# The FFN down product of a 1280-token layer: twenty output tiles of 22 blocks each, or seven block products

## The chip, the cores and the metric

The kernel runs on one core of one Trainium2 chip. The metric is the time of one execution on the device in microseconds (us). Engines are named as in the profile: PE is TensorE's matmul, PEld its weight load, DVE VectorE, ACT ScalarE, POOL GpSimd, SP the engine on whose queue the kernel puts its DMAs.

## The reference

One encoder layer and a final norm, for two sequences of 256 and 1024 tokens, 1280 tokens in all, of width 1024, in fp32:

```
h = _rmsnorm(x, norm_mix_g);  proj = h @ w_in
y_hy = _hyena(...);  y_att = _attention(...)
x = x + concat(norms of both) @ w_out
h = _rmsnorm(x, norm_ffn_g)
x = x + (silu(h @ w_gate) * (h @ w_up)) @ w_down
return _rmsnorm(x, final_norm_g)
```

w_gate and w_up are 1024 x 2816, w_down is 2816 x 1024. The change concerns the last product, the residual add and the final norm, and what of the gate/up stage feeds them.

## The kernel before

Every matmul operand is split into a high and a low part of a reduced fp32 format (`F32R`). `mm3` (line 178) makes one fp32 product of three matmuls: high by high (line 180), high by low (181), low by high (182). A split is a cast on ScalarE for the high part and a subtract for the low part, by the helper `tt` (line 173), on GpSimd where G is passed and on VectorE otherwise.

The layer up to w_out takes the span up to about 890 us; the change does not touch it. It leaves the residual sum of each of ten 128-token tiles in DRAM (`x2d`), and its normed form in SBUF.

The gate/up stage (lines 1220 to 1326) computes h @ w_gate and h @ w_up together by seven block products (Winograd's form of Strassen's scheme): `right_side` transposes the tokens and makes the seven right factors, kept in SBUF for all 1280 tokens; `left_side(n)` loads four 256 KB pieces of the weights for column block n of 22, makes four sums on GpSimd and splits seven left factors; `gate_up(n)` runs seven keys, each over two token chunks of 256 and 384 columns, four contraction blocks of three matmuls, and folds each result into the buffers s, g, t, u of 128x640 (640 tokens are one half of each token pair). At the end t and u hold the activations of one column block for the two token halves and go to DRAM in `actd` (line 1323).

The down stage (lines 1332 to 1383) runs two halves h of the 1024 output columns. For h it loads 22 blocks of w_down of 128x512 (`load_down`, raw in three buffers, 24 split ones), and for each of ten token tiles the activations of all 22 blocks from `actd` (`load_act`, two pieces of 11 blocks, 704 KB each). One PSUM bank collects 22 x 3 matmuls. VectorE then adds the residual, ScalarE squares with a row sum, and in the second half GpSimd makes the row's factor, VectorE scales both halves and SP stores them.

PSUM has eight banks in one rotating tag (`bank`, line 1217). The order of instructions on each engine's queue is fixed when the program is built, by a scheduler that runs over the program text in order and may move an instruction ahead of earlier ones where its model of the time has it ready sooner; at run time each queue is strictly in order. Inside `opened` pools a tag has a fixed number of rotating buffers, and a new tile waits for the readers of the one whose buffer it takes.

Of the kernel before, what the change touches and what calls it, by code (L numbers as in the profile page):

```python
# [11 lines left out]
F32 = mybir.dt.float32  # L12
F32R = mybir.dt.float32r
AF = mybir.ActivationFunctionType
ALU = mybir.AluOpType
# [10 lines left out]
NF = FF // 128  # L26
# [3 lines left out]
EPS = 1e-6  # L30
# [7 lines left out]
MUL, ADD, SUB = ALU.mult, ALU.add, ALU.subtract  # L38
# [77 lines left out]
def hymba_layer_kernel(ctx: ExitStack, tc: tile.TileContext, A, dbg=None):  # L116
    nc = tc.nc
    dbg = dbg or {}
    V, S, G, T, Q = nc.vector, nc.scalar, nc.gpsimd, nc.tensor, nc.sync

    cst = ctx.enter_context(tc.tile_pool(name="cst", bufs=1))
    drm = ctx.enter_context(tc.tile_pool(name="drm", bufs=1, space=DRAM))

    def opened(name, side=None, **kw):

        st = ExitStack()
        if side:
            kw["side"] = side
        return st.enter_context(tc.tile_pool(name=name, bufs=1, reuse_waits="tile", **kw)), st.close
# [12 lines left out]
    s2, r2, s1, fh = pool("s2", 8), pool("r2", 3), pool("s1", 5), pool("fh", 2)  # L142
    ca, cb, c8, t3, sm = pool("ca", 2), pool("cb", 2), pool("c8", 2), pool("t3", 2), pool("sm", 6)
# [25 lines left out]
    def stt(out, in0, scalar, in1, op0=MUL, op1=ADD, eng=None):  # L169
        (eng or V).scalar_tensor_tensor(out=out, in0=in0, scalar=scalar, in1=in1, op0=op0, op1=op1)  # L170

    def tt(out, in0, in1, op, eng=None):
        return (eng or V).tensor_tensor(out=out, in0=in0, in1=in1, op=op)  # L173

    def f(ap):
        return ap.bitcast(F32)

    def mm3(out, lh, ll, rh, rl, first, last):

        T.matmul(out=out, lhsT=lh, rhs=rh, start=first, stop=False)  # L180
        T.matmul(out=out, lhsT=lh, rhs=rl, start=False, stop=False)  # L181
        T.matmul(out=out, lhsT=ll, rhs=rh, start=False, stop=last)  # L182
# [5 lines left out]
    one = cst.tile([128, 2], F32, name="one")  # L188
    V.memset(one, 1.0)
    ones = one[:, 0:1].broadcast_to([128, 128])  # L190
    mhalf = cst.tile([128, 8], F32, name="mhalf")
# [28 lines left out]
    x1d = [drm.tile([128, 1024], F32, name=f"x1d{i}") for i in range(10)]  # L220
    x2d = [drm.tile([128, 1024], F32, name=f"x2d{i}") for i in range(10)]

    actd = drm.tile([2, 5, 128, NF, 128], F32, name="actd")
    dft = {}

    anchor = [None]
# [286 lines left out]
    def o_rows(i):  # L513
        return A["y_sample"][0, i * 128:(i + 1) * 128, :] if i < 8 else A["y_prompt"][0, (i - 8) * 128:(i - 7) * 128, :]
# [702 lines left out]
    def bank(name):  # L1217
        return psf.tile([128, 512], F32, name=name, tag="bank", bufs=8)
# [44 lines left out]
    def left_side(n):  # L1263

        cs = slice(n * 128, (n + 1) * 128)
        raw = {}
        for nm, src, k0 in (("a11", wg, 0), ("a12", wg, 4), ("a21", wu, 0), ("a22", wu, 4)):
            raw[nm] = wo0.tile([128, 4, 128], F32, name=nm, tag=nm)
            Q.dma_start(out=raw[nm], in_=src[:, k0:k0 + 4, cs])

        def parts(key, x, of):
            w = of.tile([128, 2, 4, 128], F32R, name="w" + key, tag="w" + key)
            S.copy(out=w[:, 0], in_=x)  # L1273
            tt(w[:, 1], x, f(w[:, 0]), SUB, G)
            return w

        def combo(x, y, op):
            t = wo1.tile([128, 4, 128], F32, name="ws", tag="ws", bufs=3)
            tt(t, x, y, op, G)
            return t  # L1280

        A_ = {"b11": parts("b11", raw["a11"], wo0), "b21": parts("b21", raw["a12"], wo0)}
        s1_ = combo(raw["a21"], raw["a22"], ADD)
        s2_ = combo(s1_, raw["a11"], SUB)
        A_["s2"] = parts("s2", s2_, wo0)
        A_["s3"] = parts("s3", combo(raw["a11"], raw["a21"], SUB), wo1)
        A_["s1"] = parts("s1", s1_, wo1)
        A_["b22"] = parts("b22", combo(raw["a12"], s2_, SUB), wo1)
        A_["t4"] = parts("t4", raw["a22"], wo1)
        return A_  # L1290

    def gate_up(n, by_chunk):
        W = left_side(n)
        v = {x: wo1.tile([128, 640], F32, name=f"v{x}", tag=f"v{x}", bufs=2) for x in "sgtu"}
        steps = [(c, key) for c in range(2) for key in RIGHT] if by_chunk else \
            [(c, key) for key in RIGHT for c in range(2)]
        for c, key in steps:
            c0, w = CW2[c]
            p = bank("prod")[:, 0:w]
            for k in range(4):  # L1300
                mm3(p, W[key][:, 0, k], W[key][:, 1, k], B[key][0][c][:, k], B[key][1][c][:, k], k == 0, k == 3)
            s, g, t, u = (v[x][:, c0:c0 + w] for x in "sgtu")
            if key == "b11":
                S.copy(out=s, in_=p)
            elif key == "b21":
                tt(g, p, s, ADD)
                S.activation(out=g, in_=g, func=AF.Silu)
            elif key == "s2":
                tt(s, p, s, ADD)
            elif key == "s3":  # L1310
                tt(t, p, s, ADD)
            elif key == "s1":
                tt(u, p, t, ADD)
                tt(s, p, s, ADD)
            elif key == "b22":
                tt(s, p, s, ADD)
                S.activation(out=s, in_=s, func=AF.Silu)
                tt(u, s, u, MUL)
            else:
                tt(t, t, p, SUB)  # L1320
                tt(t, g, t, MUL)
        for x, half in (("u", 1), ("t", 0)):
            Q.dma_start(out=actd[half, :, :, n].rearrange("j p t -> p j t"), in_=v[x].rearrange("p (j t) -> p j t", j=5))

    for n in range(NF):
        gate_up(n, n == 0)
    wo1_close()
    wo0_close()
    bt_close()


    dn, dn_close = opened("dn")
    gl = dn.tile([128, 1024], F32, name="gl", tag="gl")
    Q.dma_start(out=gl, in_=A["final_norm_g"].rearrange("(o d) -> o d", o=1).broadcast_to([128, 1024]))
    y0, ms0 = {}, {}

    def load_down(n, h):
        raw = dn.tile([128, 512], F32, name="draw", tag="draw", bufs=3)
        Q.dma_start(out=raw, in_=A["w_down"][0, n * 128:(n + 1) * 128, h * 512:(h + 1) * 512])
        w = dn.tile([128, 2, 512], F32R, name="wd", tag="wd", bufs=24)  # L1340
        S.copy(out=w[:, 0], in_=raw)  # L1341
        tt(w[:, 1], raw, f(w[:, 0]), SUB, G)
        return w

    def load_act(half, j):
        raw = dn.tile([128, NF, 128], F32, name="araw", tag="araw", bufs=2)
        a = dn.tile([128, 2, NF, 128], F32R, name="act", tag="act", bufs=2)
        for m in range(0, NF, 11):
            ms = slice(m, m + 11)
            Q.dma_start(out=raw[:, ms], in_=actd[half, j, :, ms])  # L1350
            S.copy(out=a[:, 0, ms], in_=raw[:, ms])  # L1351
            tt(a[:, 1, ms], raw[:, ms], f(a[:, 0, ms]), SUB)
        return a

    for h in range(2):
        hs = slice(h * 512, (h + 1) * 512)
        W = None
        for j in range(5):
            for half in range(2):
                i = 2 * pairs[j] + half  # L1360
                a = load_act(half, j)
                if W is None:
                    W = [load_down(n, h) for n in range(NF)]
                p = bank("dn")
                for n in range(NF):
                    mm3(p, a[:, 0, n], a[:, 1, n], W[n][:, 0], W[n][:, 1], n == 0, n == NF - 1)
                if h == 0:
                    y = y0[i] = dn.tile([128, 512], F32, name="y0", tag="y0", bufs=10)
                    ms0[i] = dn.tile([128, 2], F32, name="ms", tag="ms", bufs=10)
                else:  # L1370
                    y = dn.tile([128, 512], F32, name="y1", tag="y1", bufs=2)
                Q.dma_start(out=y, in_=x2d[i][:, hs])
                tt(y, p, y, ADD)
                junk = dn.tile([128, 512], F32, name="yj", tag="yj", bufs=1)
                S.activation(out=junk, in_=y, func=AF.Square, accum_out=ms0[i][:, h:h + 1])
                if h == 1:
                    r = dn.tile([128, 1], F32, name="yr", tag="yr", bufs=2)
                    tt(r, ms0[i][:, 0:1], ms0[i][:, 1:2], ADD, G)
                    G.tensor_scalar(out=r, in0=r, scalar1=1.0 / 1024, scalar2=EPS, op0=MUL, op1=ADD)
                    tt(r, r, mhalf[:, 0:1], ALU.pow, G)  # L1380
                    for z, (yy, zs) in enumerate(((y0[i], slice(0, 512)), (y, hs))):
                        stt(yy, yy, r, gl[:, zs], MUL, MUL)
                        Q.dma_start(out=o_rows(i)[:, zs], in_=yy)
    dn_close()
    psf_close()

# [23 lines left out]
```

## Time and profile before

| | us |
|---|---|
| median of three runs | 1813.91 (1812.72 to 1815.08) |
| profiled execution | 1812.55 |
| its span in the profile | 1810.3 |
| PE busy | 1654.0 (91%) |
| POOL busy | 853.7 (47%) |
| DVE busy | 963.4 (53%) |
| ACT busy | 717.8 (40%) |
| mean granted TensorE clock | 0.956 of full |

The span is what the trace covers; 2.25 us lie around it. Busy time of an engine is a sum over its instructions, and its share is an average over stages. A releaser is the instruction whose semaphore ended a wait. Matmul durations in the trace overlap, so the rate of matmuls is read from the distance of repeating events.

### The profile page before, as it was taken

To read this page: it belongs to the slowest core of one execution; us is meant where nothing else is said; L and a number is where in the kernel's file an instruction comes from. 1 tells how busy PE (TensorE), PEld (TensorE's weight loads), DVE (VectorE), ACT (ScalarE), POOL (GpSimd) and SP (SyncE) were. 2 spreads that over 40 slices of the span, in tenths; PEclk is the share of its full clock that TensorE was granted. 3 is DMA by queue.
4 is the path that set the end of the run, shared out by engine and by line. 5 is a ranking of instruction groups with operands and counts; after the bars stand their busy time and mean duration, and the time that the engine had idled before them with its cause. 6 is when DMAs were issued, how large, how long until landed. Compare 5 with 4: busy or idle time off the path is not lost.

```text
span 1810.3 us, 25721 instructions
## 1 busy us (share of the span) xinstructions
PE 1654.0 (91%) x9737; PEld 1472.9 (81%) x9737; DVE 963.4 (53%) x1514; ACT 717.8 (40%) x1331; POOL 853.7 (47%) x771
## 2 busy tenths in 40 slices
PE   6999999988796879988699999999999958999998
PEld 4777789977785868876589999999999946888786
DVE  6559889768878765564554333334333331222432
ACT  5444443336676675463342222222222223223321
POOL 5134465632778753333576555555565415005210
PEclk9899999989898979999799999999999979999999
DMA  7453445524342433332222222222222175224441
GB/s 267 150 175 104 141 136 154 169 77 129 105 140 81 125 95 136 109 143 80 73 62 64 69 71 76 65 77 69 64 76 71 41 265 179 96 96 162 156 142 58
DMA packets 158565, 205.75 MB, mean 114 GB/s; under 512 B 10960, under 2 KB 114568, under 8 KB 158283
## 3 DMA queue, kind: packets, MB, share of 16 engines
q1 hardware_dynamic: 158203, 196.25, 33.5%
q0 software_dynamic: 240, 7.86, 1.2%
q8 instruction: 77, 1.26, 0.3%
q14 instruction: 45, 0.37, 0.1%
HBM read 158.20 MB, written 53.74 MB: 117 GB/s over the span
## 4 chain that ended last, share of the span: by engine, by line
PE 44%; DMA 4%; POOL 1%; DVE 1%; ACT 1%; issue 0%; SPq 0%; POOLq 0%; DVEq 0%; ACTq 0%
PE prod L182 10%; PE prod L181 10%; PE prod L180 10%; PE dn L182 5%; PE dn L181 5%; PE dn L180 4%; DMA draw<-in_w_down 3%; POOL wd L173 1%; DMA y<-x2d 0%; ACT wd L1341 0%; PE tp L1236 0%; PE wo L182 0%; PE wo L180 0%; DVE xx L170 0%; PE wo L181 0%
## 5 line engine op out<-in xcount | busy, mean ns | idle before, releaser
L180 PE MATMUL dn<-wd,act 128*128 128x512 f32 x440 | 173.4, 400 | 22.2 <-ACT wd L1341 19.5
L181 PE MATMUL dn<-wd,act 128*128 128x512 f32 x440 | 176.5, 401 | 3.0 <-POOL wd L173 2.8
L182 PE MATMUL dn<-wd,act 128*128 128x512 f32 x440 | 175.3, 399 | 1.9 <-DVE act L173 1.9
L173 POOL TENSOR_TENSOR wd<-draw,wd 128x512 fp32r<-128x512 f32 x44 | 59.9, 1381 | 179.0 <-ACT wd L1341 175.6
L173 DVE TENSOR_TENSOR y<-dn,y 128x512 f32<-128x512 f32 x20 | 13.7, 691 | 216.6 <-PE dn L182 175.3
L1351 ACT CAST act<-araw 128x1408 fp32r<-128x1408 f32 x40 | 52.9, 1371 | 171.0 <-PE dn L182 157.9
L180 PEld LDWEIGHTS dn<-wd,act 128*128 128x128 f32 x440 | 85.0, 194 | 42.4 <-ACT wd L1341 21.1
L811 PE MATMUL pt<-ident,P 128*128 128x128 f32 x544 | 85.6, 287 | 34.2 <-DVE PT L173 25.7
L173 DVE TENSOR_TENSOR PT<-pt,PT 128x512 fp32r<-128x512 f32 x136 | 92.6, 685 | 38.4 <-ACT PT L814 37.9
L173 POOL TENSOR_TENSOR ws<-ws,ws 128x512 fp32r<-128x512 f32 x66 | 85.4, 1295 | 55.5 <-ACT ws L1273 55.5
L173 DVE TENSOR_TENSOR vs<-prod,vs 128x256 f32<-128x256 f32 (+1 forms) x132 | 64.4, 488 | 88.1 <-PE prod L182 88.1
L1273 ACT CAST ws<-ws 128x512 fp32r<-128x512 f32 x66 | 41.0, 621 | 168.9 <-PE prod L182 164.7
L814 ACT CAST PT<-pt 128x512 fp32r<-128x512 f32 x136 | 79.6, 589 | 67.8 <-PE pt L811 66.3
L181 PEld LDWEIGHTS dn<-wd,act 128*128 128x128 f32 x440 | 84.7, 192 | 26.5 <-POOL wd L173 9.4
L811 PEld LDWEIGHTS pt<-ident,P 128*128 128x128 f32 x544 | 66.3, 147 | 47.1 <-DVE PT L173 28.0
L182 PEld LDWEIGHTS dn<-wd,act 128*128 128x128 f32 x440 | 84.9, 193 | 20.0 <-DVE act L173 2.7
L828 PE MATMUL ro<-PT,V 128*128 128x256 f32 x544 | 81.2, 305 | 10.4 <-DVE PT L173 7.8
L828 PEld LDWEIGHTS ro<-PT,V 128*128 128x128 f32 x544 | 75.7, 209 | 16.2 <-DVE PT L173 10.5
L173 POOL TENSOR_TENSOR ws<-a,a 128x512 f32<-128x512 f32 x44 | 56.8, 1290 | 62.5 <-DMA a<-in_w_up 62.4
L796 DVE TENSOR_REDUCE nm<-s 128x1 f32<-128x1024 f32 (+1 forms) x68 | 82.4, 1212 | 4.4 <-PE s L792 2.7
L800 ACT ACTIVATE P<-s,nm 128x1024 f32<-128x1024 f32 (+1 forms) x80 | 79.5, 1001 | 9.8 <-DVE nm L796 9.7
L173 DVE TENSOR_TENSOR vg<-prod,vs 128x256 f32<-128x256 f32 (+1 forms) x44 | 21.6, 491 | 115.3 <-PE prod L182 114.8
(405 smaller groups left out, 5437.2 us busy)
## 6 DMA issues: line engine op xcount, KB each, us to landing
araw<-actd SPq DMA_DIRECT2D x40, 704.0 KB
tabf<-dft SPq DMA_DIRECT2D x40, 384.0 KB
a<-in_w_gate SPq DMA_DIRECT2D x44, 256.0 KB
a<-in_w_up SPq DMA_DIRECT2D x44, 256.0 KB
draw<-in_w_down SPq DMA_DIRECT2D x44, 256.0 KB
wraw<-in_w_in SPq DMA_DIRECT2D x36, 256.0 KB
dft<-in_dft POOLq DMA_DIRECT2D x5, 1536.0 KB, 9.5
tabs<-dft SPq DMA_DIRECT2D x20, 384.0 KB
```

The costliest lines, as they stand in the source:

```text
L173: return (eng or V).tensor_tensor(out=out, in0=in0, in1=in1, op=op)
L180: T.matmul(out=out, lhsT=lh, rhs=rh, start=first, stop=False)
L181: T.matmul(out=out, lhsT=lh, rhs=rl, start=False, stop=False)
L182: T.matmul(out=out, lhsT=ll, rhs=rh, start=False, stop=last)
L796: V.tensor_reduce(out=nm, in_=sf.rearrange("p (g k) -> p g k", g=n), axis=AX.X, op=ALU.max, negate=True)
L800: S.activation(out=P[:, ks], in_=sf[:, ks], func=AF.Exp, bias=nm[:, g:g + 1], accum_out=un["rs"][:, g, b:b + 1])
L811: T.transpose(out=pt[:, t * 128:(t + 1) * 128], in_=P[:, (t0 + t) * 128:(t0 + t + 1) * 128], identity=ident)
L814: S.copy(out=dh, in_=pv)
L828: T.matmul(out=o, lhsT=vt, rhs=PT[:, hl, t0 + n], start=n == 0 and hl == 0, stop=n == len(ts) - 1 and hl == 1)
L1273: S.copy(out=w[:, 0], in_=x)
L1351: S.copy(out=a[:, 0, ms], in_=raw[:, ms])
```

## The change

The down product too is computed with seven block products. The contraction (22 blocks) is halved into j and 11 + j, the tokens into the two halves, the output columns into two of 512. After each pair of column blocks j, 11 + j `down_left` makes four sums of activation blocks on VectorE and stores seven left factors of 128x640 per j to DRAM (`ad`), and `down_right` loads the four quarters of w_down's blocks in two column pieces of 256, makes four differences on GpSimd and stores them to DRAM (`td`). In gate/up two sums are made in place, the s and g buffers are single and the sums' buffers two. The down stage runs seven products; each loads, for each of 11 contraction blocks, one right factor of 128x512 and one left factor of 128x640, splits both, and runs five token tiles of three matmuls into five PSUM banks, the contraction index outermost. The last product has the token tile outermost. The results are folded into five 128x512 buffers each of s, g, t, u; the residual is added on GpSimd.

```diff
@@ -220,7 +220,9 @@
     x1d = [drm.tile([128, 1024], F32, name=f"x1d{i}") for i in range(10)]
     x2d = [drm.tile([128, 1024], F32, name=f"x2d{i}") for i in range(10)]
 
-    actd = drm.tile([2, 5, 128, NF, 128], F32, name="actd")
+    KD = NF // 2
+    ad = {o: drm.tile([KD, 128, 640], F32, name=f"ad{o}") for o in ("a11", "a12", "a22", "s1", "s2", "s3", "s4")}
+    td = {o: drm.tile([KD, 128, 512], F32, name=f"td{o}") for o in ("t1", "t2", "t3", "t4")}
     dft = {}
 
     anchor = [None]
@@ -1274,8 +1276,8 @@
             tt(w[:, 1], x, f(w[:, 0]), SUB, G)
             return w
 
-        def combo(x, y, op):
-            t = wo1.tile([128, 4, 128], F32, name="ws", tag="ws", bufs=3)
+        def combo(x, y, op, out=None):
+            t = wo1.tile([128, 4, 128], F32, name="ws", tag="ws", bufs=2) if out is None else out
             tt(t, x, y, op, G)
             return t
 
@@ -1283,15 +1285,15 @@
         s1_ = combo(raw["a21"], raw["a22"], ADD)
         s2_ = combo(s1_, raw["a11"], SUB)
         A_["s2"] = parts("s2", s2_, wo0)
-        A_["s3"] = parts("s3", combo(raw["a11"], raw["a21"], SUB), wo1)
+        A_["s3"] = parts("s3", combo(raw["a11"], raw["a21"], SUB, raw["a21"]), wo1)
         A_["s1"] = parts("s1", s1_, wo1)
-        A_["b22"] = parts("b22", combo(raw["a12"], s2_, SUB), wo1)
+        A_["b22"] = parts("b22", combo(raw["a12"], s2_, SUB, s2_), wo1)
         A_["t4"] = parts("t4", raw["a22"], wo1)
         return A_
 
     def gate_up(n, by_chunk):
         W = left_side(n)
-        v = {x: wo1.tile([128, 640], F32, name=f"v{x}", tag=f"v{x}", bufs=2) for x in "sgtu"}
+        v = {x: wo1.tile([128, 640], F32, name=f"v{x}", tag=f"v{x}", bufs=2 if x in "tu" else 1) for x in "sgtu"}
         steps = [(c, key) for c in range(2) for key in RIGHT] if by_chunk else \
             [(c, key) for key in RIGHT for c in range(2)]
         for c, key in steps:
@@ -1319,68 +1321,159 @@
             else:
                 tt(t, t, p, SUB)
                 tt(t, g, t, MUL)
-        for x, half in (("u", 1), ("t", 0)):
-            Q.dma_start(out=actd[half, :, :, n].rearrange("j p t -> p j t"), in_=v[x].rearrange("p (j t) -> p j t", j=5))
-
-    for n in range(NF):
-        gate_up(n, n == 0)
+        return v["t"], v["u"]
+
+    def down_left(j, one, two):
+
+        (a11, a21), (a12, a22) = one, two
+
+        def sum_(x, y, op, key, out=None):
+            t = wo1.tile([128, 640], F32, name="vx", tag="vx", bufs=2) if out is None else out
+            tt(t, x, y, op)
+            Q.dma_start(out=ad[key][j], in_=t)
+            return t
+
+        for key, x in (("a11", a11), ("a12", a12), ("a22", a22)):
+            Q.dma_start(out=ad[key][j], in_=x)
+        x1_ = sum_(a21, a22, ADD, "s1")
+        x2_ = sum_(x1_, a11, SUB, "s2")
+        sum_(a11, a21, SUB, "s3", a21)
+        sum_(a12, x2_, SUB, "s4")
+
+    def down_right(j):
+
+        for q in range(2):
+            b = {}
+            for nm, n, h in (("b11", j, 0), ("b12", j, 1), ("b21", KD + j, 0), ("b22", KD + j, 1)):
+                b[nm] = wo1.tile([128, 256], F32, name="d" + nm, tag="d" + nm)
+                c = h * 512 + q * 256
+                Q.dma_start(out=b[nm], in_=A["w_down"][0, n * 128:(n + 1) * 128, c:c + 256])
+            t1, t2 = (wo1.tile([128, 256], F32, name=f"dt{z}", tag=f"dt{z}") for z in range(2))
+            for key, out, x, y in (("t1", t1, b["b12"], b["b11"]), ("t3", b["b12"], b["b22"], b["b12"]),
+                                   ("t2", t2, b["b22"], t1), ("t4", b["b21"], t2, b["b21"])):
+                tt(out, x, y, SUB, G)
+                Q.dma_start(out=td[key][j, :, q * 256:(q + 1) * 256], in_=out)
+
+    for j in range(KD):
+        one = gate_up(j, j == 0)
+        down_right(j)
+        two = gate_up(KD + j, False)
+        down_left(j, one, two)
     wo1_close()
     wo0_close()
     bt_close()
 
 
+
     dn, dn_close = opened("dn")
...
+    wd = A["w_down"][0]
+    straight = {"b11": (0, 0), "b21": (KD, 0), "b22": (KD, 1)}
+
+    def parts2(x, tag, width, eng):
+        w = dn.tile([128, 2, width], F32R, name=tag, tag=tag, bufs=KD + 3)
+        S.copy(out=w[:, 0], in_=x)
+        tt(w[:, 1], x, f(w[:, 0]), SUB, eng)
         return w
 
...
+    def factors(left, right, k):
+        b = dn.tile([128, 512], F32, name="dbr", tag="dbr", bufs=3)
+        if right in straight:
+            n, h = straight[right]
+            Q.dma_start(out=b, in_=wd[(n + k) * 128:(n + k + 1) * 128, h * 512:(h + 1) * 512])
+        else:
+            Q.dma_start(out=b, in_=td[right][k])
+        a = dn.tile([128, 640], F32, name="dar", tag="dar", bufs=3)
+        Q.dma_start(out=a, in_=ad[left][k])
+        return parts2(b, "dbf", 512, G), parts2(a, "daf", 640, V)
+
+    def product(left, right, by_tile, done):
+        F_ = {}
+        order = [(t, k) for t in range(5) for k in range(KD)] if by_tile else \
+            [(t, k) for k in range(KD) for t in range(5)]
+        p = {}
+        for t, k in order:
+            if k not in F_:
+                F_[k] = factors(left, right, k)
+            if t not in p:
+                p[t] = bank("dn")
+            b, a = F_[k]
+            ts = slice(t * 128, (t + 1) * 128)
+            mm3(p[t], a[:, 0, ts], a[:, 1, ts], b[:, 0], b[:, 1], k == 0, k == KD - 1)
+            if k == KD - 1:
+                done(t, p[t])
+
+    gl = []
+    v2 = {x: [] for x in "sgtu"}
+    ms2 = {}
+
+    def residual(x, t, half, h):
+
+        xr = dn.tile([128, 512], F32, name="xr2", tag="xr2", bufs=3)
+        Q.dma_start(out=xr, in_=x2d[2 * pairs[t] + half][:, h * 512:(h + 1) * 512])
+        tt(x[t], x[t], xr, ADD, G)
+
+    def squares(x, t, half, h):
+        if (t, half) not in ms2:
+            ms2[t, half] = dn.tile([128, 2], F32, name="ms2", tag="ms2", bufs=10)
+        junk = dn.tile([128, 512], F32, name="yj", tag="yj", bufs=2)
+        S.activation(out=junk, in_=x[t], func=AF.Square, accum_out=ms2[t, half][:, h:h + 1])
+
+    def finished(t, half, left, right):
+        if not gl:
+            gl.append(dn.tile([128, 1024], F32, name="gl", tag="gl"))
+            Q.dma_start(out=gl[0], in_=A["final_norm_g"].rearrange("(o d) -> o d", o=1).broadcast_to([128, 1024]))
+        m = ms2[t, half]
+        r = dn.tile([128, 1], F32, name="yr", tag="yr", bufs=2)
+        tt(r, m[:, 0:1], m[:, 1:2], ADD, G)
+        G.tensor_scalar(out=r, in0=r, scalar1=1.0 / 1024, scalar2=EPS, op0=MUL, op1=ADD)
+        tt(r, r, mhalf[:, 0:1], ALU.pow, G)
+        i = 2 * pairs[t] + half
+        for h, x in enumerate((left, right)):
+            hs = slice(h * 512, (h + 1) * 512)
+            stt(x[t], x[t], r, gl[0][:, hs], MUL, MUL)
+            Q.dma_start(out=o_rows(i)[:, hs], in_=x[t])
+
+    def new(x):
+        t = dn.tile([128, 512], F32, name=f"y{x}", tag=f"y{x}", bufs=5)
+        v2[x].append(t)
+        return t
+
+    def p1(t, p):
+        S.copy(out=new("s"), in_=p)
+
+    def p2(t, p):
+        tt(new("g"), p, v2["s"][t], ADD)
+        residual(v2["g"], t, 0, 0)
+        squares(v2["g"], t, 0, 0)
+
+    def p6(t, p):
+        tt(v2["s"][t], p, v2["s"][t], ADD)
+
+    def p7(t, p):
+        tt(new("t"), p, v2["s"][t], ADD)
+
+    def p5(t, p):
+        tt(new("u"), p, v2["t"][t], ADD)
+        tt(v2["s"][t], p, v2["s"][t], ADD)
+        residual(v2["u"], t, 1, 1)
+        squares(v2["u"], t, 1, 1)
+        residual(v2["s"], t, 0, 1)
+        residual(v2["t"], t, 1, 0)
+
+    def p3(t, p):
+        tt(v2["s"][t], p, v2["s"][t], ADD)
+        squares(v2["s"], t, 0, 1)
+        finished(t, 0, v2["g"], v2["s"])
+
+    def p4(t, p):
+        tt(v2["t"][t], v2["t"][t], p, SUB)
+        squares(v2["t"], t, 1, 0)
+        finished(t, 1, v2["t"], v2["u"])
+
+    for left, right, by_tile, done in (("a11", "b11", False, p1), ("a12", "b21", False, p2), ("s2", "t2", False, p6),
+                                       ("s3", "t3", False, p7), ("s1", "t1", False, p5), ("s4", "b22", False, p3),
+                                       ("a22", "t4", True, p4)):
+        product(left, right, by_tile, done)
     dn_close()
     psf_close()
 
```

## Rows read from the trace of the kernel before

**Rows 1.** The page's part 1: busy time, share of the span, instructions.
```profile
PE 1654.0 (91%) x9737; PEld 1472.9 (81%) x9737; DVE 963.4 (53%) x1514; ACT 717.8 (40%) x1331; POOL 853.7 (47%) x771
```

**Rows 2.** Busy time by stretch: PE, PEld, DVE, ACT, POOL, granted clock, DMA share, GB/s.
```profile
963.00:1404.00 441.00, 441.00 (x3013) 441.00 (x3013) 167.16 (x323) 123.34 (x233) 256.29 (x198) 1.00 0.24 71
1460.97:1802.70 341.73, 314.67 (x1320) 252.75 (x1320) 92.87 (x79) 91.45 (x122) 76.93 (x71) 0.95 0.43 151
1461.00:1473.00 12.00, 0.00 (x0) 0.00 (x0) 3.15 (x4) 3.20 (x4) 0.00 (x0) 0.61 0.84 291
1473.00:1522.00 49.00, 38.79 (x131) 27.15 (x132) 5.00 (x3) 16.21 (x25) 29.02 (x23) 0.82 0.70 258
1573.51:1633.35 59.84, 59.84 (x265) 49.55 (x264) 15.41 (x13) 13.07 (x17) 0.00 (x0) 1.00 0.27 97
1802.50:1810.30 7.80, 0.18 (x1) 0.00 (x0) 2.10 (x3) 0.72 (x2) 0.94 (x3) 0.66 0.18 67
```

**Rows 3.** Timeline of DVE, down stage: start, duration, instruction (first and last of five).
```profile
1573.51 0.69 DVE L173 TENSOR_TENSOR y<-dn,y 128x512 f32<-128x512 f32 x1 [10.39 <-PE dn L182]
...
1633.35 0.69 DVE L173 TENSOR_TENSOR y<-dn,y 128x512 f32<-128x512 f32 x1 [10.39 <-PE dn L182]
```

**Rows 4.** Groups of the down stage: busy, mean ns of one, idle before by releaser.
```profile
L180 PE MATMUL dn<-wd,act 128*128 128x512 f32 x440 | 173.4, 400 | 22.2 <-ACT wd L1341 19.5 <-ACT act L1351 2.7
...
L173 POOL TENSOR_TENSOR wd<-draw,wd 128x512 fp32r<-128x512 f32 x44 | 59.9, 1381 | 179.0 <-ACT wd L1341 175.6 <-DMA draw<-in_w_down 3.4
...
L1341 ACT CAST wd<-draw 128x512 fp32r<-128x512 f32 x44 | 27.0, 620 | 55.7 <-DMA draw<-in_w_down 48.5 <-PE dn L182 4.6 <-POOL wd L173 2.1
...
L173 DVE TENSOR_TENSOR y<-dn,y 128x512 f32<-128x512 f32 x20 | 13.7, 691 | 216.6 <-PE dn L182 175.3 <-issue 41.3
```

**Rows 5.** Chain of waits, start of the down stage: start, duration, engine or transfer.
```profile
1473.18 7.53 DMA y<-x2d
...
1480.77 6.38 DMA draw<-in_w_down
...
1496.42 2.59 DMA draw<-in_w_down
...
1499.09 0.63 ACT wd L1341
...
1499.79 1.30 POOL wd L173
...
1526.84 0.43 PE dn L180
...
1531.53 0.43 PE dn L182
...
1532.20 0.23 PE dn L181
```

**Rows 6.** Timeline of SP's queue, start of the down stage: start, duration, issues.
```profile
1465.40 1.72 SPq L1339 DMA_DIRECT2D draw<-in_w_down  x3
...
1469.44 10.23 SPq L1372 DMA_DIRECT2D y<-x2d  x11
```

**Rows 7.** Timeline of DVE and POOL in the gate/up stage.
```profile
1433.63 1.30 POOL L173 TENSOR_TENSOR wb<-ws,wb 128x512 fp32r<-128x512 f32 x1 [2.24 <-ACT wb L1273]
...
1434.01 1.33 DVE L173 TENSOR_TENSOR vu<-vs,vu 128x384 f32<-128x384 f32 x1 [0.60 <-ACT vs L1317]
...
1436.96 0.56 DVE L173 TENSOR_TENSOR vt<-vg,vt 128x384 f32<-128x384 f32 x1
...
1437.11 1.55 POOL L173 TENSOR_TENSOR wt<-a,wt 128x512 fp32r<-128x512 f32 x1 [2.18 <-ACT wt L1273]
```

**Rows 8.** Timeline of ACT in the down stage.
```profile
1573.51 2.65 ACT L1351 CAST act<-araw 128x1408 fp32r<-128x1408 f32 x2 [11.69 <-PE dn L182]
1576.06 0.63 ACT L1375 ACTIVATE yj<-y 128x512 f32<-128x512 f32 x1
```

**Rows 9.** Group of POOL, whole span: a 256-column subtract.
```profile
L173 POOL TENSOR_TENSOR M<-M 128x256 f32<-128x256 f32 x40 | 29.7, 750 | 43.9 <-DVE M L173 43.1
```

More of the change, by code (lines that the diff above doesn't have):

```diff
@@ L1332, in hymba_layer_kernel @@
     dn, dn_close = opened("dn")
[L1333 to L1342, printed above, removed]
-        return w
@@ L1345, in load_act @@
[L1345 to L1383, printed above, removed]
```

## The prediction

> **What bounds the kernel now.** I read four views in this order. First the page's totals: TensorE is busy 91% of the span and no other engine over 53% [rows 1]; that is an average over stages, so next come the stretches. In the gate/up stage TensorE has no gap: 441.0 us busy of 441.0 in nine steady pairs of column blocks, 49.0 us a pair, with POOL busy 256 us and VectorE 167 us beside it [rows 2]. The last gate/up product ends near 1461.0. The down stage runs from there to 1802.7, 341.7 us, and is two different things [rows 2]: from 1461 to 1473 no matmul at all with the DMA engines at 84%, from 1473 to 1522 a starved TensorE at a granted clock of 0.82, and after that a fed one. Fed, one output tile of 66 matmuls takes 14.96 us: VectorE's first PSUM read of five stands at 1573.51 and its last at 1633.35, 59.84 us for four tiles [rows 3], so a 512-column matmul costs 14.96/66 = 0.2267 us. (The 400 ns of a group's mean [rows 4] are latencies that overlap; the spacing is the price.) 1320 x 0.2267 = 299.2 us, so 341.7 - 299.2 = 42.5 us of the old stage are not matmul time: most lies before 1522, where the first tile needs all 22 weight blocks, the rest where the second half's weights are loaded. The chain there goes draw load 2.59, cast 0.63, POOL subtract 1.30 us, over three buffers [rows 5].
>
> **The change, part by part.** Against the profiled execution's 1812.55 us, which is 1.36 below the median of the three runs.
>
> *Matmuls of the down stage.* Twenty tiles x 22 x 3 = 1320 become 7 products x 11 x 5 x 3 = 1155 of the same shape: 1155 x 0.2267 = 261.8 us. Against the old 299.2 that is -37.4.
>
> *The start of the stage.* The old one loses 42.5 us to loading. The new first product needs one weight block and one activation block to start, and 15 matmuls, 3.40 us, use them before the next pair is needed. Before the first matmul: the last VectorE sum s4 behind the final multiply (estimate 0.9, below), its store's issue and two loads' issues on SP (1.7, at 0.57 each as three draw issues in a row took 1.72 [rows 6]), a load of 2.59, casts of 0.63 and some 0.78, while only the low part's matmul waits for the subtract: 6.6, about 7 us. The old stage shows 12 us of gap; bounds 5 and 12, I take 7, because the new first load is 256 KB where the old first was 704 KB. After the starved stretch the chain has twelve matmuls at 0.43 us, the 1.2 GHz level, before 0.23, the 2.4 GHz one, comes back [rows 5]: 12 x 0.20 = 2.4 us, taken once. So 9.4 in place of most of 42.5.
>
> *Supply inside a product.* Each k step needs a weight block of 256 KB (ScalarE cast 0.62, POOL subtract 1.30) and an activation block of 320 KB (cast 0.62 x 640/512 = 0.78, VectorE subtract 0.56 x 640/384 = 0.93, scaled from shorter forms [rows 4, 7]). Per step POOL 1.38 by its mean [rows 4], ScalarE 1.40, VectorE 0.93, all under 3.40. One weight slot's cycle 2.59+0.63+1.30 = 4.5 us over three buffers is a step every 1.5 us; with the 6.38 us that a load took in the crowd before 1487 [rows 5] it is (6.38+0.63+1.30)/3 = 2.8 us, still under 3.40. So the 14 slots of finished factors fill up within the first products; then the factors are three steps or more ahead. Cost 0, cover: the 3.40 us of matmuls.
>
> *The six seams between products.* Each product's five banks finish within one step; the next one has three free banks and needs the others 2 us later, while one VectorE read of PSUM takes 0.69 [rows 4]. Unseen in the trace is whether the next factors are queued ahead of these reads. Program order alone would put them behind; but the queues are not in program order: SP issued y loads in a row between 1469 and 1480 whose tiles come much later [rows 6], and ScalarE casts the next activations ahead of the squares of the tile that has just ended [rows 8]. Bounds: 0, and 10.4 us a seam (five reads 3.5, chain 4.5, slow clock 2.4). I take 1 us each, near the lower end since the hoisting rows are of this very loop: 6.0.
>
> *Residual adds.* Twenty of 128x512 move from VectorE to POOL, five after the second product and fifteen after the fifth, at 1.30 each: 6.5 and 19.5 us on POOL, with the loads behind three buffers and the squares on ScalarE waiting on them. If the factors are a dozen steps (40 us) ahead, nothing; if not, up to 26 us. I take 0.
>
> *Gate/up stage.* Per pair POOL gains 8 subtracts of 256 columns, 0.75 each [rows 9]: 6.0 on 28.5 of 49.0 [rows 2], 34.5. VectorE gains four 640-column sums, about 0.9 each, on 18.6. SP gains 8 loads and 8 stores of 128 KB and three more stores (seven for four) a pair, 19 x 0.57 = 10.8 us; POOL and SP have the room. The in-place sums hold two buffers longer: a21's is free only after s3's subtract, two products or 7 us later (a block of 24.5 us has seven), and its next content is wanted in the block after; I cost that at 0, with a block as the cover. Where the single s and g buffers make a writer wait, eight PSUM banks stand between it and TensorE. Cover: TensorE's 49.0 us a pair. At the stage's start, where the first weights are split while TensorE wants them, I add 2 us, an estimate; bounds 0 and 6.0 (one pair's subtracts).
>
> VectorE and POOL do get in each other's way here: a 384-column multiply takes 1.33 us where POOL's subtract began before it and 0.56 where it began first, and then POOL's subtract takes 1.55 for 1.30 [rows 7].
> The Trainium skill (SBUF — State Buffer, "Who interferes with whom") says that a VectorE instruction with two SBUF inputs and a POOL instruction that reads SBUF shut each other out for the whole instruction, and the two pairs agree in kind. By that rule the new sums and subtracts would run one after another, which is the second rival's condition below.
>
> *End.* The last tile's read, squares, three POOL instructions, two scalings and the store are the same: 7.8 us [rows 2], no difference. The last product goes tile by tile and wants eleven factors in its first 11 x 3 x 0.2267 = 7.5 us; with 14 slots its last factor's slot is free after the eighth step of the product ahead, 10 us before that ends. 0; if it is late all the same, eleven blocks at 1.5 us less 7.5 make 9.
>
> Sum of the stage: 261.8 + 7.0 + 2.4 + 6.0 = 277.2 for 341.7, -64.5; gate/up +2.0; 1812.55 - 62.5 = **1750.0 us**.
>
> **The rivals.**
> *First, seams drained in queue order (slower).* Place: ScalarE, VectorE and SP at each of the six seams. If the finishing reads, squares and residual loads stand ahead of the next factors, each seam costs 10.4, 62.4 in all, and the 26 us of residual adds come on top since no lead exists: 88.4 in place of 6.0, so 1750 + 82.4 = 1832. It turns the sign from 68.5 us of waits at the seams on (62.5 and the 6.0 counted). For it: the finishing code stands first in the program. Against: the hoisting [rows 6, 8]. 8%.
> *Second, POOL and VectorE become the bound of gate/up.* If all of POOL's 34.5 and VectorE's work with two SBUF inputs (8 multiplies of at most 0.56, 4.5, plus the sums' 3.7) ran one after another, that is 43 of 49.0 us, still covered; only if the bursts of 6.0 per pair land on weights that are due would all eleven show: 66 us, so 1816, no measurable change. 4%.
> *Third, only the residual burst shows.* 26 us, 1776. For it: ScalarE's squares wait for POOL and the casts stand in the same queue. Against: the 40 us lead. 17%.
> *Fourth, the start gains less than it says.* A hoisted row of residual loads and the final gain's load delays the first blocks, as y loads did for 7.53 us in the old chain [rows 5]: 8 to 15 us, about 1762. 6%; inside the range anyway.
> *Fifth, every k step waits for its pair and TensorE stays at the slow level.* 15 x 0.43 = 6.45 us a step, 77 x 3.05 = 235 more, 1985. Against: with fed queues the stretch from 1573 shows granted clock 1.00 [rows 2], and supply is 1.5 to 2.8 us a step. 2%.
> [...]
>
> **How the numbers follow.** The forecast has 63%, its own range 1738 (gap 5, seams 0, slow clock 0, gate/up 0 and rounding) to 1768 (gap 12, seams 2.5 each, gate/up 6). With the third and fourth rivals the range reaches 1738 to 1783; outside it lie the first, second and fifth and the forecast's edges. About 0.2% is what a measurement of this kernel can tell from no change. Faster: forecast, third, fourth and part of the second, 0.88; same 0.03; slower (first, fifth, rest of the second) 0.09.
>
> **What would show it.** After: 1155 down matmuls at 0.227 us spacing; a gap near 7 us at the end of gate/up; no TensorE wait over 1 us at the seams; gate/up pairs still at 49.0 us. Seam waits behind ScalarE or VectorE would show the first rival; a POOL residual row as releaser of TensorE the third; gate/up pairs longer than 49.0 the second; granted clock below 0.9 through the stage the fifth.

## The result, and the profile after

The changed kernel takes 1758.07 us, median of 4 runs (1754.86 to 1761.85), against 1813.88 for the kernel before: ratio 0.9693, 95% interval [0.9672, 0.9714]. The forecast was 1750, the range 1738 to 1783. The profiled execution took 1756.95 us.

The page of the changed kernel, its part 1:

```profile
span 1755.0 us, 26505 instructions
...
PE 1611.2 (92%) x9572; PEld 1444.5 (82%) x9572; DVE 1064.5 (61%) x1610; ACT 735.4 (42%) x1406; POOL 993.7 (57%) x912
```

Against [rows 1] TensorE has 43 us less work, POOL 140 and VectorE 101 us more. Where the time went is read from the stretches (columns as in [rows 2]): four of the gate/up stage, most of the gap, then five of the seven products in their order, the end.

```profile
966.00:1015.00 49.00, 49.00 (x337) 49.00 (x336) 27.75 (x41) 11.28 (x23) 36.42 (x37) 1.00 0.55 181
...
1064.00:1113.00 49.00, 46.09 (x313) 45.48 (x313) 21.89 (x37) 12.53 (x26) 45.15 (x42) 1.00 0.62 198
1113.00:1162.00 49.00, 44.88 (x293) 44.07 (x292) 23.06 (x37) 12.57 (x26) 36.69 (x31) 0.97 0.45 145
...
1260.00:1309.00 49.00, 49.00 (x337) 49.00 (x336) 22.39 (x41) 13.63 (x27) 28.42 (x23) 1.00 0.28 91
...
1474.50:1482.60 8.10, 0.00 (x0) 0.00 (x0) 2.25 (x4) 1.34 (x2) 0.97 (x1) 0.61 0.91 311
1482.60:1525.00 42.40, 42.35 (x178) 34.66 (x178) 23.50 (x20) 26.20 (x40) 29.33 (x21) 0.95 0.92 311
1525.00:1560.00 35.00, 34.35 (x152) 28.24 (x152) 19.71 (x17) 20.30 (x34) 21.11 (x16) 1.00 0.78 255
1560.00:1600.00 40.00, 40.00 (x178) 33.14 (x177) 22.24 (x21) 18.38 (x34) 22.79 (x17) 1.00 0.67 210
...
1675.00:1712.00 37.00, 37.00 (x165) 30.65 (x164) 18.66 (x20) 15.29 (x32) 34.80 (x28) 1.00 0.56 184
1712.00:1747.20 35.20, 35.20 (x157) 29.09 (x155) 14.17 (x21) 3.62 (x10) 8.95 (x22) 1.00 0.36 134
1747.20:1755.00 7.80, 0.36 (x2) 0.00 (x0) 2.10 (x3) 0.72 (x2) 0.93 (x3) 0.85 0.18 67
```

The down stage is an almost unbroken stream of matmuls, at full clock after its first product, with POOL at 35 of 37 us beside it where the residual adds fall (1675 to 1712). The gap before it is 8.8 us (the first of the waits below). But the gate/up stage, which had no gap from 963 to 1404 before [rows 2], now has two stretches in which TensorE stands for 3 and 4 us, and POOL's extra work and the transfers all lie in its first part: 36 to 45 us of POOL and a DMA share of 0.45 to 0.62 until 1162, then 28.4 and 0.28, near the 28.5 and 0.24 of before the change. What TensorE waited for, from 912 us on:

```profile
PE dn L180 <- ACT daf L1374: 8.8, 1, 8.8
PE prod L180 <- DVE vt L173: 3.6, 2, 2.1
PE prod L180 <- ACT vs L1306: 3.3, 2, 1.9
PE prod L180 <- ACT ws L1275: 3.2, 2, 1.7
PE dn L180 <- ACT ys L1442: 0.6, 1, 0.6
...
```

The row of 3.2 us behind `ws` stands in the kernel before too. New are 3.6 and 3.3 us behind the reads of PSUM in gate/up; the 0.6 is all that the six seams cost. The waits are not the whole price in gate/up: the two stretches from 1064 to 1162 hold 313 and 293 matmuls where a full one holds 337, and 68 matmuls fewer are worth 9.9 us at 337 in 49.0. The granted clock is 0.97 in the second.

To compare kernels I measure gate/up from the first to the last matmul of line 180 with key b11, whose last stands 21.8 us ahead of the stage's end. In the view by tile of `prod` that is one row, its first and last start; here before and after:

```profile
L180 PE MATMUL prod<-b11h,wb x176: 277/334/386, 914.6 to 1439.2; 128*128 128x256 f32 x88, 128*128 128x384 f32 x88
```

```profile
L180 PE MATMUL prod<-b11h,wb x176: 278/334/386, 916.9 to 1452.0; 128*128 128x256 f32 x88, 128*128 128x384 f32 x88
```

524.6 and 535.1 us. (The expectations below count to the stage's end instead, which adds some 22 us: their 546 and 558.) So the span's change of 55.3 us adds up as: 2.3 later at the first block (the work ahead of it is not touched; in the ten profiles of this study the first block starts anywhere from 914.6 to 923.4), 10.5 longer gate/up, 3.2 less from there to the first down matmul (33.9 to 30.7), 64.7 less from that to the end of the last (329.6 to 264.9), 0.2 less behind it (7.6 to 7.4): 2.3 + 10.5 - 3.2 - 64.7 - 0.2 = -55.3.

### The profile page after: what moved, and what is told of

Its sections match the earlier page's. It is cut to its first block, busy times and chain, and to the rows that moved or that the text cites. A ratio compares the mean times of both kernels' runs of the same rounds, so it can differ in the third digit from the quotient of the medians.

```text
span 1755.0 us, 26505 instructions
## 1 busy us (share of the span) xinstructions
PE 1611.2 (92%) x9572; PEld 1444.5 (82%) x9572; DVE 1064.5 (61%) x1610; ACT 735.4 (42%) x1406; POOL 993.7 (57%) x912
## 5 line engine op out<-in xcount | busy, mean ns | idle before, releaser
L173 POOL TENSOR_TENSOR dbf<-dbr,dbf 128x512 fp32r<-128x512 f32 x77 | 108.6, 1413 | 118.5 <-ACT dbf L1374 115.4
L173 DVE TENSOR_TENSOR daf<-dar,daf 128x640 fp32r<-128x640 f32 x77 | 101.0, 1313 | 106.4 <-ACT daf L1374 105.1
L180 PE MATMUL dn<-dbf,daf 128*128 128x512 f32 x385 | 149.7, 393 | 9.5 <-ACT daf L1374 8.8
L181 PE MATMUL dn<-dbf,daf 128*128 128x512 f32 x385 | 149.4, 391 | 0.0
L182 PE MATMUL dn<-dbf,daf 128*128 128x512 f32 x385 | 147.8, 389 | 0.0
L813 PE MATMUL pt<-ident,P 128*128 128x128 f32 x544 | 86.4, 291 | 33.7 <-DVE PT L173 26.0
L180 PEld LDWEIGHTS dn<-dbf,daf 128*128 128x128 f32 x385 | 72.8, 189 | 25.4 <-ACT daf L1374 9.2
L173 DVE TENSOR_TENSOR vu<-vs,vu 128x256 f32<-128x256 f32 (+1 forms) x44 | 42.5, 965 | 80.9 <-ACT vs L1319 80.9
L1374 ACT CAST dbf<-dbr 128x512 fp32r<-128x512 f32 x77 | 47.9, 622 | 99.3 <-issue 46.7
L181 PEld LDWEIGHTS dn<-dbf,daf 128*128 128x128 f32 x385 | 73.0, 190 | 15.3
L1275 ACT CAST ws<-ws 128x512 fp32r<-128x512 f32 x44 | 27.3, 620 | 139.0 <-POOL ws L173 76.7
L182 PEld LDWEIGHTS dn<-dbf,daf 128*128 128x128 f32 x385 | 72.3, 188 | 15.1
L181 PE MATMUL us<-al,wh 128*128 128x512 f32 x192 | 77.4, 403 | 1.2 <-DVE al L173 1.2
L180 PE MATMUL wo<-woh,yhi 128*128 128x512 f32 x160 | 66.6, 420 | 11.8 <-ACT yhi L1079 9.1
```

What stands on the lines that cost most here:

```text
L813: T.transpose(out=pt[:, t * 128:(t + 1) * 128], in_=P[:, (t0 + t) * 128:(t0 + t + 1) * 128], identity=ident)
```

## The experiments

**Spread the differences.** Theory: the extra 10 us of gate/up come from `down_right`, of which the scheduler drew all eleven ahead. Rival: the in-place sums, the single buffers and `down_left`.

```diff
-            Q.dma_start(out=raw[nm], in_=src[:, k0:k0 + 4, cs])
+            loaded[0] = Q.dma_start(out=raw[nm], in_=src[:, k0:k0 + 4, cs])
...
-        down_right(j)
+        with tc.issue_after(loaded[0].ins):
+            down_right(j)
```

> Edit: the loads and stores that down_right puts on SP's queue are queued behind the last weight load of the same pair's first block, so that the eleven right-hand differences are spread over the gate/up stage and no longer all issued in its first five pairs. Theory A (the gate/up stage grew from 546 to 558 us because all 88 quarter-block loads and 88 stores were issued between 912 and 1131 us, and the gate/up weight loads stood behind loads that waited for a store to land): gate/up back to about 547 to 549 us, 9 to 11 us less, time about 1748. Rival B (the in-place sums, the single s and g buffers and the sums of down_left on VectorE made the stage longer): gate/up still near 558, time about 1757.

Measured: 1747.63 us, ratio to before 0.9638 [0.9622, 0.9655], below and clear of the changed kernel's interval. The loads of w_down's quarters, first and last issue, in the changed kernel and here:

```profile
L1350 SPq DMA_DIRECT2D db<-in_w_down x88: 327/422/1836, 912.3 to 1122.3; - x88
```

```profile
L1352 SPq DMA_DIRECT2D db<-in_w_down x88: 327/422/1242, 911.2 to 1407.9; - x88
```

```profile
L180 PE MATMUL prod<-b11h,wb x176: 278/334/387, 915.8 to 1441.0; 128*128 128x256 f32 x88, 128*128 128x384 f32 x88
```

The same loads over 497 us in place of 210, and gate/up is 525.2 us, 0.6 more than before the change; the five stretches from 966 to 1211 show TensorE at 49.00 of 49.00, POOL at 33.7 to 35.6. All of this kernel's sums, in-place buffers and stores are still there, so the rival falls.

**Leave the differences out.**

```diff
-        down_right(j)
...
-    straight = {"b11": (0, 0), "b21": (KD, 0), "b22": (KD, 1)}
+    straight = {"b11": (0, 0), "b21": (KD, 0), "b22": (KD, 1), "t1": (0, 1), "t2": (0, 0), "t3": (KD, 1), "t4": (KD, 0)}
```

> Edit: down_right is left out, and the four products that used its differences take blocks of w_down as they are (so the output columns are not the reference's). Same matmuls, same loads in the down stage. Theory A: with no differences at all the gate/up stage is 546 to 548 us, time 1746 to 1748. Rival B (in-place sums, single buffers, down_left): gate/up stays near 558, time about 1757. A third reading, POOL's 66 us of extra subtracts as such: e2 gains and e1 does not.

Measured: 1749.66 us, ratio 0.9647 [0.9632, 0.9662]; gate/up from 920.7 to 1445.5, 524.8 us. With no differences it is no faster than with spread ones: their whole price is in where they were put.

**Which half of them holds gate/up up?** One kernel keeps the transfers and drops POOL's subtracts, the other keeps the subtracts on tiles loaded once.

```diff
-            t1, t2 = (wo1.tile([128, 256], F32, name=f"dt{z}", tag=f"dt{z}") for z in range(2))
-            for key, out, x, y in (("t1", t1, b["b12"], b["b11"]), ("t3", b["b12"], b["b22"], b["b12"]),
-                                   ("t2", t2, b["b22"], t1), ("t4", b["b21"], t2, b["b21"])):
-                tt(out, x, y, SUB, G)
+            for key, out in (("t1", b["b11"]), ("t3", b["b12"]), ("t2", b["b22"]), ("t4", b["b21"])):
                 Q.dma_start(out=td[key][j, :, q * 256:(q + 1) * 256], in_=out)
```

> Edit: down_right keeps its 88 loads and 88 stores on SP's queue, not spread, but without the four subtracts on POOL (the stored right factors are plain blocks of w_down, so the outputs are not the reference's). If what lengthens gate/up is SP's queue standing behind loads that wait for a store to land out of the same single buffer: gate/up still 553 to 558 us. If it is the 66 us of POOL subtracts drawn into the first five pairs: gate/up 546 to 548.

```diff
...
+                if nm not in held:
+                    held[nm] = wo1.tile([128, 256], F32, name="d" + nm, tag="d" + nm)
+                    Q.dma_start(out=held[nm], in_=A["w_down"][0, n * 128:(n + 1) * 128, h * 512:h * 512 + 256])
+                b[nm] = held[nm]
...
                 tt(out, x, y, SUB, G)
-                Q.dma_start(out=td[key][j, :, q * 256:(q + 1) * 256], in_=out)
...
```

> Edit: the other half: the 88 subtracts of 256 columns stay on POOL, on tiles loaded once, with no further loads and no stores (the products take plain blocks of w_down, so the outputs are not the reference's). SP's queue as the cause: gate/up 546 to 548 us, time about 1748. POOL's subtracts as the cause: gate/up 553 to 558 us.

Measured: transfers alone 1756.63 us, gate/up 916.3 to 1452.6, 536.3; subtracts alone 1756.79 us, gate/up 919.1 to 1449.3, 530.2. The first theory had SP's queue as all of it; each half alone does harm, and the two prices (11.7 and 5.6 us) add up to more than the changed kernel's 10.5. Transfers alone cost one hole of 6.8 us, subtracts alone two of 2.7 and 1.7. Stretches 1015 to 1064 of the first and 1064 to 1113 of the second:

```profile
1015.00:1064.00 49.00, 41.69 (x267) 41.05 (x266) 22.37 (x33) 12.25 (x25) 29.12 (x21) 0.90 0.69 223
```

```profile
1064.00:1113.00 49.00, 44.59 (x302) 44.07 (x301) 27.87 (x34) 11.07 (x23) 45.13 (x43) 1.00 0.26 84
```

The three kernels share a long chain of waits. Waits of other engines in gate/up, in the changed kernel and in the spread one, where it is short:

```profile
DVE vu L173 <- ACT vs L1319: 79.8, 42, 11.4
ACT ws L1275 <- POOL ws L173: 76.7, 10, 17.7
...
SPq L1350 <- DMA tdt<-db: 36.8, 33, 3.1
```

```profile
DVE vu L173 <- ACT vs L1321: 23.8, 44, 0.6
ACT ws L1277 <- POOL ws L173: 13.8, 5, 3.8
```

A cast on ScalarE waits up to 17.7 us for a late sum on POOL; the silu of the running block stands behind that cast in ScalarE's queue, VectorE's multiply waits up to 11.4 us for the silu, the PSUM reads stand behind the multiply, and TensorE runs out of banks. (The two waits are up to 16.7 and 8.2 us with transfers alone, 11.7 and 7.9 with subtracts alone.) POOL's sum is late because POOL is full (subtracts alone, 45 of 49 us), or because its weight load stands in SP's queue among loads that wait for a store out of the same single buffer (transfers alone, where POOL waits up to 15.1 us for a weight; in the changed kernel the row `tdt<-db`, 36.8 us, shows SP's share).

What stands directly ahead of the holes differs. With transfers alone it is the store of one of `down_left`'s sums: the sum is made at 1030.3, its store leaves SP's queue only at 1042.60, behind loads and stores of w_down's pieces, and the fourth sum, which takes its buffer, waits 8.78 us with the PSUM reads behind it on VectorE:

```profile
1045.25 0.82 DVE L173 TENSOR_TENSOR vx<-vt,vx 128x640 f32<-128x640 f32 x1 [8.78 <-DMA ads<-vx]
```

```profile
1042.60 2.55 DMA ads<-vx
1045.41 0.57 issue
1045.99 0.43 DVE vg L173
1046.46 0.58 PE prod L180
```

With subtracts alone, a multiply on VectorE had waited 7.91 us for its silu and then took 7.87 us, where the same form takes 0.43 elsewhere; eight instructions of POOL lie over it without a break, from 1075.17 to 1082.96:

```profile
1075.38 7.87 DVE L173 TENSOR_TENSOR vu<-vs,vu 128x256 f32<-128x256 f32 x1 [7.91 <-ACT vs L1319]
...
1083.77 0.44 PE L180 MATMUL prod<-s2h,ws 128*128 128x384 f32 x1 [2.71 <-DVE vs L173]
```

In the changed kernel the second hole of each of the two stretches stands behind three sums of `down_left`, which reach VectorE late by the long chain and take 4.3 us beside POOL's subtracts, for 2.5 alone; two of the second stretch's, and the hole:

```profile
1135.65 1.57 DVE L173 TENSOR_TENSOR vx<-vu 128x640 f32<-128x640 f32 x1
...
1138.58 1.91 DVE L173 TENSOR_TENSOR vx<-vx,vt 128x640 f32<-128x640 f32 x1
...
1141.74 0.58 PE L180 MATMUL prod<-s1h,ws 128*128 128x256 f32 x1 [2.10 <-DVE vt L173]
```

How the changed kernel's 10.5 us divide between late sums, late stores and operations that VectorE and POOL lengthen for each other was not separated.

**Eight plain products in the new order.** How much of the gain is the smaller number of matmuls, how much the new order of the work?

```diff
-        order = [(t, k) for t in range(5) for k in range(KD)] if by_tile else \
-            [(t, k) for k in range(KD) for t in range(5)]
+        order = [(t, k) for k in range(cut) for t in range(5)] + [(t, k) for t in range(5) for k in range(cut, NF)]
...
+    for x, half, h in (("s", 0, 0), ("g", 0, 1), ("t", 1, 0), ("u", 1, 1)):
+        product(half, h, x == "u", quarter(x, half, h))
```

Here `cut` is 22, and 11 in the last product, whose second half goes tile by tile; `quarter` copies the bank on ScalarE and adds the residual on POOL.

> Edit: the new down stage with its outer contraction loop over five banks and its factors from DRAM, but as eight plain block products (four output quarters of 22 steps) instead of seven; no sums, no differences. 1320 matmuls. If the terms of the sum are right: matmuls 1320 x 0.2267 = 299.2 in place of 261.8, +37.4; gate/up without sums and differences 546 to 548, -10 to -11; time about 1784, that is 29 us under the kernel before, all of it from the stage's start. Rival (the start was not what was gained, the matmuls were nearly all of it): time near 1805 to 1813.

Measured: 1787.32 us, ratio 0.9863 [0.9845, 0.988]. From the first down matmul to the last:

```profile
1474.20:1776.00 301.80, 301.80 (x1320) 249.45 (x1320) 130.62 (x106) 133.80 (x231) 160.95 (x134) 0.99 0.62 203
```

301.8 against the old stage's 329.6 with the same 1320 matmuls, and a gap of 7.8 us against 12: 32 us less in the stage. The time is 25 us under the kernel before, not 32: in this profile the first gate/up block began 5.4 us later (920.0 for 914.6) and the end took 1.4 longer. So the rival falls: the new order and layout of the stage, with no sum of factors anywhere, gives some 25 us of the time, and seven products for eight take another 37 from the stage (301.8 to 264.9).

**Take the hoisting away at the seams.**

```diff
-        product(left, right, by_tile, done)
+        with ExitStack() as st:
+            for ins in list(last.values()):
+                st.enter_context(tc.issue_after(ins.ins))
+            product(left, right, by_tile, done)
```

Here `last` holds the last PSUM read on VectorE and the last copy or square on ScalarE of the product before.

> Edit: at each of the six seams the next product's casts on ScalarE and subtracts on VectorE are queued behind the last read of PSUM and the last square of the product before (issue order only). If the hoisting of the factors is what keeps the seams free, each seam now shows the last read 0.7, a cast of 0.62 and one of 0.72, the wait for a raw pair behind three buffers, and the slow clock: 3 to 10 us a seam, 18 to 60 in all, more after the fifth product whose squares wait for POOL; time 1775 to 1818. If the seams cost nothing for another reason (five banks, short reads), time about 1757.

Measured: 1802.85 us, ratio 0.9939 [0.9924, 0.9954]: 45 us of the gain are gone. What TensorE waited for from 1490 us on:

```profile
PE dn L180 <- ACT daf L1374: 31.1, 4, 18.2
```

The four waits are not alike. The first seam, where five copies of PSUM stand ahead of the casts on ScalarE, shows 1.8 us, the second 6.9, the fifth 18.2, the sixth 4.1; the third and fourth, whose banks VectorE alone reads, show none. (There ScalarE has nothing that the next casts could be queued behind, so the edit holds back VectorE's subtracts alone.) The longest is after the fifth product, where fifteen residual adds stand on POOL, the squares wait for them on ScalarE, and the casts behind the squares; the matmuls after it run slow again:

```profile
1573.79 2.50 PE L180 MATMUL dn<-dbf,daf 128*128 128x512 f32 x5 [6.94 <-ACT daf L1374]
...
1707.07 2.50 PE L180 MATMUL dn<-dbf,daf 128*128 128x512 f32 x5 [18.17 <-ACT daf L1374]
```

```profile
ACT yj L1421 <- POOL yu L173: 34.8, 5, 20.9
...
ACT yj L1421 <- POOL yg L173: 20.6, 5, 17.9
```

From the first down matmul to the last it takes 308 us against 265: 31 us of these waits, 2 behind subtracts, and the rest at the slow level, the granted clock of the stage being 0.93 for 0.99. The second and fifth seams, where squares wait for residual adds, hold 25 of the 31 us.

**The last product with the contraction outermost.**

```diff
-                                       ("a22", "t4", True, p4)):
+                                       ("a22", "t4", False, p4)):
```

> Edit: the last product too with the contraction index outermost, so that its five tiles end together. The prediction set the end at no difference because the last product goes tile by tile. If that is what keeps it: after the last matmul VectorE has five reads of 0.69 and ten scalings of 0.75, 11 us in place of 2.2, so the end grows from 7.8 us to some 14 to 17 and the time by 6 to 9 us, to about 1765. If the end is set by something else (the store's landing, POOL's three instructions): within 2 us of 1757.

Measured: 1760.52 us, ratio 0.97 [0.9669, 0.9731], not to be told from the changed kernel by the times. In its profile the stretch after the last matmul is longer:

```profile
1742.20:1754.40 12.20, 0.00 (x1) 0.00 (x0) 7.63 (x12) 1.59 (x6) 6.82 (x13) 0.64 0.57 215
```

This stretch begins at the last matmul's end: 12.2 us, where the changed kernel has 7.4. So the tile order of the last product is worth some 4.8 us, less than the 6 to 9 expected: when the last matmul ended, four of the five reads were done or under way, and the ten scalings followed, most of them 0.67 us apart. Its gate/up took 531.2 us, with the same order on every queue there as the changed kernel, which took 535.1, and the kernel of the seams, which took 532.2; the hold-up differs from one execution to the next, which hides 4.8 us in the times.

**Three steps ahead.** The start of the down stage is a chain behind the last gate/up block. Here the first three steps of the first product use raw and split buffers that this block has finished with, and the differences are spread.

```diff
+    for k in range(AHEAD):
+        b, a, c = early(k)
+        for t in range(5):
+            if t not in p_first:
+                p_first[t] = bank("dn")
+            lh, ll = (a[:, z, t * 128:(t + 1) * 128] if t < 4 else c[:, z] for z in range(2))
+            mm3(p_first[t], lh, ll, b[:, 0], b[:, 1], k == 0, False)
     wo1_close()
```

> Edit: the spread differences of the earlier run, and the first three steps of the first product made from buffers of the gate/up stage (raw and split weight buffers that its last block no longer needs), traced before the stage's memory is given back. If the stage's start is a chain of store issue, load, cast in a row behind the last gate/up product, three steps of 3.4 us cover it: the gap of about 8 to 9 us goes and with it the slow clock's 2.4, so 8 to 11 us under the spread version, 1737 to 1740. If the fourth step is late instead, or the early casts hold up the last gate/up block: less than 4 us of gain, 1744 or more.

Measured: 1735.74 us, ratio 0.9551 [0.9524, 0.9577], the fastest of all, 11.9 us under the spread version, a little more than the 8 to 11 expected. From the first gate/up block to the end the two profiles differ by 11.2 us (827.5 and 816.3). The 30 us around the end of gate/up have no hole and full clock:

```profile
1455.00:1485.00 30.00, 30.00 (x157) 26.49 (x156) 14.44 (x23) 9.50 (x16) 7.78 (x6) 1.00 0.67 242
```

## Why the prediction was right, and which terms were off

- *Matmuls of the down stage*, 1155 x 0.2267 = 261.8: from the first to the last there are 264.9 us, which hold the slow clock's 2.4 and the seams' 0.6. The eight-product run has the same price: 301.8 less 2.4 is 299.4 for 299.2.
- *The start*, a gap of 7 and 2.4 of slow clock: 8.8 and about 2.5. The chain of sums, store issue, load and cast was the right one; the first load left SP at 1477.25, 3.3 us after the last gate/up matmul, where I had counted 1.5. The three-steps run removes the gap whole.
- *Supply inside a product*: right, no step waited. But VectorE's subtract took 1313 ns on average, not 0.93 us, and POOL's 1413. The rows:

```profile
L173 POOL TENSOR_TENSOR dbf<-dbr,dbf 128x512 fp32r<-128x512 f32 x77 | 108.6, 1413 | 118.5 <-ACT dbf L1374 115.4
L173 DVE TENSOR_TENSOR daf<-dar,daf 128x640 fp32r<-128x640 f32 x77 | 101.0, 1313 | 106.4 <-ACT daf L1374 105.1
```

  The two subtract beside each other from SBUF and hold each other up, as in [rows 7]; 3.40 us a step covers it. The Trainium skill (SBUF — State Buffer, "Who interferes with whom") has this as mutual exclusion of two-input VectorE work and POOL's reads; the shortest of these VectorE subtracts took 0.82 us, and so did 640-column sums of the same profile with POOL idle, so the longer mean agrees.
- *Seams*: 0.6 in place of 6.0. The reason given, hoisted factors, is shown by the run that took the hoisting away (+45 us) for the four seams where casts came to stand behind copies or squares; at the third and fourth the casts were not held back, so what they would cost is not shown. The first rival's price was 82 on top of the forecast. It was too high because the raw blocks still came early, and of its two places casts behind PSUM copies alone cost 1.8 us, squares behind residual adds 25.
- *Residual adds*: no wait of TensorE, as taken; 6.9 and 18.2 us once the lead is gone, which is the third rival's 26.
- *Gate/up*: **the term that failed**, +2.0 against +10.5. The prediction spread the new work evenly, "Per pair POOL gains 8 subtracts", 34.5 of 49.0, and concluded that POOL and SP have the room. Spread evenly the stage grows by 0.6 us, as the first experiment shows; the in-place sums and single buffers cost nothing, as taken. But `down_right` depends on nothing that gate/up makes, and the same hoisting on which the seams' term rests drew all eleven into the first five pairs. The second rival named the place and part of the condition. Two-input work that shuts itself out does show: 7.87 us of one multiply ahead of a hole with subtracts alone, and lengthened sums ahead of two holes of the changed kernel. But the weight that is late on POOL, and the queue of SP, which harms alone, were not in it.
- *The end*: 7.6 us after the last matmul before, 7.4 now. It holds because the last product goes tile by tile.
- *The fifth rival* falls: the granted clock is 0.95 in the first product, which holds the slow matmuls after the gap, and 1.00 in the other products shown, with a transfer pair under every step and a DMA share up to 0.92. Where the lead was taken away it is 0.93 over the stage.
- *The range*: its upper end of 1783 lies 7 us above the third rival's 1776, and no line of the working gives these 7.

The errors partly cancelled: the down stage with its start came out 3.5 us better than the sum (273.7 for 277.2), gate/up 8.5 worse, and 2.3 us lie ahead of the change, where the prediction has no term.

What stays open: why the hold-up in gate/up differs between executions of one queue order (531.2 to 535.1) was not tried, nor how its price divides among its causes.

## What to carry to other kernels

Making the contraction the outer loop over several PSUM banks turns a stage that must load a whole operand first into one that needs one block per step; that was worth some 25 us of the time here, beside the 37 of the saved product. A scheduler that moves work ahead helps where the work is next in line and harms where it has no tie to its neighbours: work whose inputs are ready from the start must be tied to the stage it is meant to lie in. And a stage that begins with a chain of store, load and cast can be begun in the last stage's finished buffers, here for 11.9 us.

## What was not expected of the hardware

Some rows stand out. A sum of 128x640 with both inputs in SBUF took 0.82 us where POOL was idle, and a subtract of the same size 1.31 on average beside POOL. A multiply of 128x256, 0.43 us elsewhere, took 8.05 in the changed kernel while eight instructions of POOL ran over it without a break, and 10.55 under eleven with subtracts alone; neither of these two stood ahead of a hole:

```profile
932.25 8.05 DVE L173 TENSOR_TENSOR vt<-vg,vt 128x256 f32<-128x256 f32 x1
```

```profile
1019.46 10.55 DVE L173 TENSOR_TENSOR vu<-vs,vu 128x256 f32<-128x256 f32 x1 [1.18 <-ACT vs L1319]
```

Why other multiplies came through after one instruction of POOL (1.39 us at 1129.26) is not shown. And with 311 GB/s moving under the first product TensorE stayed busy 42.35 of 42.40 us.
